# Split weight blocks whose low part comes from an accumulating DMA instead of a subtraction

## The chip, the cores and the metric

One core of one Trainium2 chip runs the whole program in one launch. The metric is the device time of that launch in microseconds; lower is better. The kernel before has three timed runs: 2505.35, 2509.59 and 2516.16 us, median 2509.59.

## What is computed

One inference step of a two-layer backbone on 640 tokens of 1,024 features (128 context tokens and 512 latent tokens). Each layer is a half-step feed-forward, a token mixing and a second half-step feed-forward, each followed by a residual and a layer norm, with shift, scale and gate vectors from two conditions:

```python
def half_ffn(x, shift, scale, gate, w_gate, w_up, w_down, g, b):
    h = modulate(x, shift, scale)
    return post_norm(x, FFN_HALF * swiglu(h, w_gate, w_up, w_down), gate, g, b)

for l in range(DEPTH):
    mc = ada_mods(c_ctx[None, :], w_ada[l], b_ada[l])
    ms = ada_mods(c, w_ada[l], b_ada[l])
    y = half_ffn(y, ...)
    o = ab_mixer(...) if l % 2 == 0 else fourier_mixer(...)
    y = post_norm(y, o, ...)
    y = half_ffn(y, ...)
```

Layer 0 mixes with two attentions (a windowed one and a latent one, with one input and one output projection), layer 1 with a Fourier transform over positions and channels. The hidden width of the feed-forward is 2,816. All data are float32.

## The kernel before

Features lie on the partitions, tokens on the free axis, in two parts of 256 and 384 tokens (later 254 and 386), of which the second goes first. A float32 product is made of three products of TensorE's float32r type: x = hi + lo with hi the rounded value and lo the rest, and w x = w_hi x_hi + w_hi x_lo + w_lo x_hi (`mm3`). So each weight block of 128 x 1,024 floats (512 KB) has to be split into hi and lo before TensorE reads it.

`load_in` takes one of **three raw tiles** (`self.raws`), issues the block's load on SyncE's queue, and starts the generator that `block` returns. That generator has two pieces: a copy of raw to hi, by ScalarE or VectorE, and then lo = raw - hi, by VectorE or GpSimd; behind the subtraction the raw tile is given back, and the pair is filed under its key. The engine of a piece is chosen by estimates (`choose`, with the prices of `copies` and `sums`).

The blocks that go this way are the 176 gate and up blocks of the four feed-forwards (`gu_block`, 44 each), their 88 down blocks, 12 of the attention's input projection and 8 of its output projection: 284. The 128 tiles of w_ada (modulation vectors) pass through the same three raw tiles, but are read in place by VectorE (two instructions CUSTOM_DVE_ANT_0 each). The Fourier mixing splits its blocks in code of its own, which the change leaves as it is.

Names in what follows: `wu` and `w` hold gate and up blocks (at the output projection also the blocks 0 to 3), `wd` down blocks (there the blocks 4 to 7), `wi` and `w` the input projection's; `hh` and `hl` are the high and low parts of the activations, `hd` those of the hidden layer. hi and lo have the same name with consecutive numbers: `wu_8991` is a hi, `wu_8992` its lo.

The order of all work is fixed when the program is written. TensorE's products stand in line (`chain`, `ffn`, `ab_out`); the other engines' pieces are generators that `tick` emits when an estimate of the clock (`Clock`, `Queue`, `Loads`) says that they can start. The engines then work through their queues in that order, each instruction waiting for what it needs. `load_in` may issue a load as soon as a raw tile has been given back in this order; on the chip the load then waits until the last reader of that tile is through.

Places in hi and lo tiles: a feed-forward has room for six gate and up blocks and four down blocks at a time, the output projection for all eight of its own (two are loaded early, during the attention).

Of the kernel before, what the change touches and what calls it, by code (L numbers as in the profile page):

```python
# [24 lines left out]
# The tokens in two parts; features are on the partitions throughout. Up to the attention the prompt and 128 of  # L25
# the sample, and the rest; then the prompt and what meets its mirror image in the sample's first or last 63, and
# the sample's first token and the others. By part: (first column, token among prompt and sample, tokens).
# [16 lines left out]
# Of the scheduling below, in ns: how far ahead of TensorE's queue the other engines' pieces are emitted, what  # L44
# speaks against DVE where a piece can go elsewhere, and what counts as the same time.
# [3 lines left out]
# Units of the two attentions in progress at once.  # L49
UNITS_A, UNITS_B = 6, 4  # L50
# The engines for the first modulation's scale, by tile: TensorE or DVE.
# [3 lines left out]
def pieces(parts, t0, n):  # L55
    """Where the tokens t0 to t0 + n lie: (part, column, tokens before, tokens)."""
    out = []
    for half, runs in enumerate(parts):
        for c, t, m in runs:
            a, b = max(t, t0), min(t + m, t0 + n)  # L60
            if a < b:
                out.append((half, c + a - t, a - t0, b - a))
    return out


class Clock:
    """Estimates in ns: by tile, when it will be written (and by which engine) and when its slot is free."""
# [5 lines left out]
class Pool:  # L73
    """A pool of tiles that notes which tile follows which in a slot; since: when its memory is free at the earliest."""
# [15 lines left out]
    def used(self, name):  # L90
        """When the last tile of that name will be through."""
        return self.clock.used.get(self.rings[name][-1], 0) if name in self.rings else 0


class Slots:
    """Tiles of one shape in a pool, taken and given back in any order."""
# [26 lines left out]
class Queue:  # L123
    """An engine, with an estimate in ns of when it will be through what it has been given."""
# [4 lines left out]
    def __getattr__(self, op):  # L129
        def issue(*args, **kw):  # L130
            aps = [x for x in (*args, *kw.values()) if isinstance(x, bass.AP)]
            out = kw.get("out", args[0] if args else None)
            self.run(aps, [out, kw.get("accum_out")], self.cost(op, args, aps, kw))
            return getattr(self.engine, op)(*args, **kw)  # L134
        return issue

# [13 lines left out]
    def after(self, x):  # L150
        """When tile x can be read."""
# [18 lines left out]
class Loads:  # L170
    """The DMA queue."""
# [14 lines left out]
def sums(n):  # L186
    """What a sum or difference of n columns takes, by the engines that it can go to."""
# [3 lines left out]
def scaled(n, times=1):  # L191
    """Likewise for n columns times a scale by partition plus a shift by partition."""
# [3 lines left out]
def copies(x, times=1):  # L196
    """Likewise for copies of x."""
# [12 lines left out]
def size(x):  # L210
    return int(np.prod(x.shape[1:]))


class Step:
    """Float32 products run as float32r: x = hi + lo with hi rounded to float32r and lo the exact rest,
    w x = w_hi x_hi + w_hi x_lo + w_lo x_hi; or as float32, where the splits would cost more than they spare.

    Instructions are issued in the order of emission. Matrix products are emitted in line; the work of the other
    engines is in generators, whose pieces `tick` emits as they are expected to start. A generator yields the
    engine of its next piece (or None) and what that waits for: a tile, or a condition on what has been emitted."""  # L220

    def __init__(self, ctx, tc, io):
# [7 lines left out]
        # what is put off of a plain normalisation, and how many tiles that leaves  # L230
# [30 lines left out]
    def parted(self, parts):  # L261
        """The tokens' parts from here on: widths, and (column, width, modulation vector), vector 0 c's, 1 c_ctx's."""
# [8 lines left out]
    def ffn_pool(self, ctx):  # L271
        """Its memory was used until now."""
# [7 lines left out]
    def psum(self, ctx):  # L280
        """A stage's banks for the products emitted in line; two more are for the generators."""
        self.banks = Slots(self.pool(ctx, "ps", space=bass.MemoryType.PSUM), "a", 6, [128, 512], F32)

    def spawn(self, gen, on=None, what=None, unit=False, first=0):
        """first: its rank among pieces that can start at the same time."""
        self.side.append([gen, on, what, unit, first])

    def begin(self, on, what):
        """When a piece is expected to start, None if it can't yet."""
# [7 lines left out]
    def choose(self, on, what):  # L297
        """The engine that is expected to be through with a piece first, and when it would start."""
# [8 lines left out]
    def step(self, limit=None, patient=False):  # L307
        """Emit the piece expected to start first; with a limit, only one that keeps to it (by engine)."""
# [9 lines left out]
        try:  # L318
            # a generator that has begun is told which engine
# [18 lines left out]
    def pair(self, n):  # L338
        """Room for two sums of n columns, in one bank where they go there."""
# [31 lines left out]
    def load_in(self, src, use):  # L371
        """Issue a load into a free raw tile; use(tile) then is spawned, or done if it is no generator."""
# [7 lines left out]
    def loader(self, loads):  # L380
        """Loads in turn, each (when it may be issued, source, use)."""
# [4 lines left out]
    def block(self, dst, key, pool, name, bufs):  # L386
        """What turns a loaded block into its (hi, lo), kept in dst[key]."""
        def use(raw):
# [3 lines left out]
            eng = yield sums(size(hi)), hi  # L392
            eng.tensor_tensor(lo, raw, hi.bitcast(F32), ALU.subtract)
            self.raws.give(raw)
# [9 lines left out]
    def products(self, out, parts, hl, start, stop):  # L404
        """out (+)= sum of v x over parts (v, columns of x), the products with x's high part first."""
# [8 lines left out]
    def chain(self, ps, w, xs, tick=True):  # L414
        """ps = sum over k of w[k] (K, M) and xs[k] (K, N), each as (hi, lo)."""
# [7 lines left out]
    def ada_open(self, ctx, early=False):  # L423
        """What the modulation vectors are worked out with: silu of both conditions, on every partition."""
# [29 lines left out]
    def rstd(self, q, n, eps, out, delta=None, banks=None):  # L454
        """out[0] = 1/sqrt(colsum(q)/n + eps), or less (colsum(delta)/n)^2 under the root, broadcast over the
        partitions in a bank; q and delta are given back."""
# [9 lines left out]
        # the last 128 columns overlap those before where need be  # L466
# [24 lines left out]
        # a first guess from the exponent, then three of Newton's steps  # L491
# [17 lines left out]
    def affine(self, i, l, m):  # L509
        """(scale, shift), [128, KT, 2] each, by which the normalised rows become the modulated ones:  # L510
        normalisation i (or none), then the modulation (l, m), (l, m + 1)."""
# [39 lines left out]
    def norm_sum(self, half, o, st, then):  # L551
        """Add output tile o to the sum over the features, in the order of o; after the last go on with then()."""
# [14 lines left out]
    def shifted_sum(self, half, o, st, then):  # L567
        """The same without waiting for all features: what comes of output tile o less the mean m of the first two
        tiles, the sum of the squares and that of the tiles after the first two. With d the mean of all the
        differences, to which the first two tiles add nothing, the variance is the mean square less d^2, and d^2 is  # L570
        at most three times the variance."""
# [24 lines left out]
    def pivot(self, half, st, s):  # L596
        """The sum of the first two tiles' features, from the tiles' sum s."""
# [10 lines left out]
    def square(self, half, st, o, n):  # L608
        """Add the square of ya[o] to the sum of squares st["q"]; with all tiles at once the last ones' sum is in st["part"]."""
# [24 lines left out]
    def norm(self, half, st, i, aff, ag, plain=False, spill=None):  # L634
        """Layer norm i of a part. Then, modulated by aff, the next stage's input, into self.h (plain: not
        split), and in ya (or spill) ALPHA times the normalised rows; without aff, the result."""
# [4 lines left out]
        # at the end there are no products that need the other banks  # L641
        banks = self.banks if aff is None and not held else self.psc
        # the mean, with the tiles shifted already what is left of it
# [75 lines left out]
    def h_split(self, half, o, t, h):  # L719
        """The next stage's input tile from t, which is given back."""  # L720
# [9 lines left out]
    def start(self, pool):  # L730
        """The first input: the modulation's shift by DVE, its scale by TensorE, a tile of features at a time."""
# [15 lines left out]
        # silu of both conditions, on every partition  # L747
# [12 lines left out]
        def weighed(o):  # L760
            # by DVE
# [40 lines left out]
        def rest():  # L802
            for o in range(KT):
                if o + 1 < KT:
                    # among the first blocks of weights
# [11 lines left out]
    def gu_block(self, l, j, n, pool, dst, turn=0):  # L817
        """Loading the n-th block of gate and up weights: 2 f + (0 or 1). Of six in turn two are kept in w."""
# [3 lines left out]
    def ffn(self, l, j, i, nxt, pool, gu, first, turn=0, ada=0, urgent=0, after=(), early=False, **kw):  # L822
        """i: the normalisation that ends it; nxt: the modulation (layer, index) that follows it; gu: the
        first blocks of weights, there or on their way; ada: how many tiles of w_ada to work through, so many of them urgent;
# [1271 lines left out]
```

## Time and profile before

| | |
|---|---|
| median of three runs | 2509.59 us (2505.35 to 2516.16) |
| profiled execution, span from its first to its last instruction | 2503.6 us, 6.0 us below the median |
| TensorE matmul, weight load | 2413.5 us (96%), 2314.1 us (92%) |
| VectorE, ScalarE, GpSimd | 1595.8 us (64%), 723.5 us (29%), 641.9 us (26%) |
| DMA | 259.03 MB, 31.0% of 16 engines' time, mean 103 GB/s |

The profile is one execution. A group's row gives its busy time and the mean of one instruction; the idle time behind the bar is that of the engine just before it, with what ended it. The share of an engine over the whole span is a mean over stages with different limits. PE stands for TensorE's products, PEld for its weight loads, DVE for VectorE, ACT for ScalarE, POOL for GpSimd, SP for SyncE.

### The profile page before, as it was taken

How to read it: one execution, taken by the hardware profiler on the slowest of the kernel's cores; microseconds unless marked ns; L12 is line 12 of the kernel's file. 1: busy time of each engine (PE TensorE's matmuls, PEld its weight loads, DVE VectorE, ACT ScalarE, POOL GpSimd, SP SyncE). 2: the span in 40 equal slices, each digit the busy share in tenths (PEclk: the TensorE clock that was granted, in tenths of full speed). 3: DMA queues.
4: the chain of work that ended last, by engine and by line, in shares of the span. 5: the costliest groups of instructions: out<-in, count | busy, mean ns of one | idle time of the engine just before them, and what ended most of it. 6: DMA issues, size and time to landing. Idle time of an engine off the chain costs nothing. (4 is left out here: it accounts for less than half of the span.)

```text
span 2503.6 us, 39511 instructions
## 1 busy us (share of the span) xinstructions
PE 2413.5 (96%) x15713; PEld 2314.1 (92%) x15713; DVE 1595.8 (64%) x3194; ACT 723.5 (29%) x1475; POOL 641.9 (26%) x499
## 2 busy tenths in 40 slices
PE   7999999989989999999999999999989989999997
PEld 7999999987577999999999999999976879999997
DVE  8867766677567686456566677676687963323346
ACT  3221212254666442112122322211234322221122
POOL 6312221242322152013112421100245522201112
PEclk8999999999899999999999999999999989999998
DMA  6535434140012225134240354443423213112121
GB/s 247 177 118 176 143 118 160 34 135 31 7 36 78 85 84 169 64 122 149 95 136 27 102 174 137 132 147 118 136 81 108 90 43 102 65 63 76 51 76 43
DMA packets 86025, 259.03 MB, mean 103 GB/s; under 512 B 13832, under 2 KB 26824, under 8 KB 85712
## 3 DMA queue, kind: packets, MB, share of 16 engines
q1 hardware_dynamic: 85840, 256.50, 31.0%
q8 instruction: 124, 2.03, 0.3%
q14 instruction: 61, 0.50, 0.1%
HBM read 248.84 MB, written 5.52 MB: 102 GB/s over the span
## 5 line engine op out<-in xcount | busy, mean ns | idle before, releaser
L359 PE MATMUL a<-hh,wu 128*128 128x254 f32 (+3 forms) x3840 | 855.1, 311 | 4.7 <-DVE hh L134 4.6
L359 PEld LDWEIGHTS a<-hh,wu 128*128 128x128 f32 x3840 | 653.4, 190 | 6.7 <-DVE hh L134 5.8
L359 PE MATMUL a<-hd,wd 128*128 128x254 f32 (+3 forms) x4224 | 629.1, 310 | 3.7 <-DVE ya L134 3.4
L359 PEld LDWEIGHTS a<-hd,wd 128*128 128x128 f32 x4224 | 624.2, 189 | 6.7 <-issue 3.7
L359 PE MATMUL a<-hl,wu 128*128 128x386 f32 (+3 forms) x1920 | 597.5, 311 | 3.0 <-POOL hl L134 1.6
L359 PE MATMUL a<-hh,w 128*128 128x254 f32 (+6 forms) x2240 | 504.2, 314 | 1.3 <-ACT hh L134 0.9
L134 DVE CUSTOM_DVE_ANT_0 junk<-raw,cond,bada 128x1024 bf16<-128x1024 f32 x256 | 379.0, 1481 | 12.3 <-DMA raw<-in_w_ada 7.8
L359 PEld LDWEIGHTS a<-hh,w 128*128 128x128 f32 (+1 forms) x2240 | 380.2, 191 | 7.1 <-issue 2.5
L359 PEld LDWEIGHTS a<-hl,wu 128*128 128x128 f32 x1920 | 364.9, 190 | 4.6 <-DVE hl L134 2.2
L134 DVE TENSOR_TENSOR tmp<-tmp,a 128x254 f32<-128x254 f32 (+3 forms) x176 | 85.5, 486 | 430.1 <-PE a L359 420.3
L359 PE MATMUL a<-hl,w 128*128 128x254 f32 (+4 forms) x1056 | 329.8, 312 | 3.0 <-POOL hl L134 2.0
L134 DVE SCALAR_TENSOR_TENSOR ya<-a,gate,ya 128x128 f32<-128x128 f32 (+3 forms) x576 | 226.7, 433 | 145.7 <-PE a L359 144.7
L134 POOL TENSOR_TENSOR wu<-raw,wu 128x1024 fp32r<-128x1024 f32 x55 | 150.4, 2744 | 633.0 <-ACT wu L134 617.0
L134 ACT CAST hd<-tmp 128x386 fp32r<-128x386 f32 (+3 forms) x163 | 75.5, 463 | 513.2 <-DVE tmp L134 513.0
L359 PEld LDWEIGHTS a<-hl,w 128*128 128x128 f32 (+1 forms) x1056 | 200.4, 190 | 6.4 <-POOL hl L134 2.8
L134 POOL TENSOR_TENSOR w<-raw,w 128x1024 fp32r<-128x1024 f32 (+3 forms) x49 | 106.9, 2189 | 357.9 <-ACT w L134 356.8
L134 ACT ACTIVATE tmp<-a 128x254 f32<-128x254 f32 (+3 forms) x176 | 76.8, 437 | 323.3 <-PE a L359 322.6
L134 ACT CAST wu<-raw 128x1024 fp32r<-128x1024 f32 x110 | 113.2, 1047 | 160.4 <-DMA raw<-in_w_gu 122.1
L134 ACT CAST wd<-raw 128x1024 fp32r<-128x1024 f32 x66 | 68.2, 1047 | 254.7 <-PE a L359 153.7
L134 DVE TENSOR_TENSOR hd<-tmp,hd 128x254 fp32r<-128x254 f32 (+3 forms) x152 | 89.3, 588 | 65.2 <-ACT hd L134 64.9
L134 POOL TENSOR_TENSOR wd<-raw,wd 128x1024 fp32r<-128x1024 f32 x22 | 60.4, 2749 | 193.7 <-ACT wd L134 150.8
L134 DVE TENSOR_TENSOR wd<-raw,wd 128x1024 fp32r<-128x1024 f32 x70 | 95.0, 1365 | 10.5 <-ACT wd L134 9.8
(438 smaller groups left out, 2575.8 us busy)
## 6 DMA issues: line engine op xcount, KB each, us to landing
raw<-in_w_gu SPq DMA_DIRECT2D x176, 512.0 KB, 3.7
raw<-in_w_ada SPq DMA_DIRECT2D x128, 512.0 KB, 3.8
raw<-in_w_dn SPq DMA_DIRECT2D x88, 512.0 KB, 3.6
raw<-in_w_fin SPq DMA_DIRECT2D x16, 520.0 KB, 3.8
wd<-in_w_ada SPq DMA_DIRECT2D x16, 512.0 KB, 7.5
raw<-in_w_ab SPq DMA_DIRECT2D x11, 512.0 KB, 3.7
raw<-in_w_abo SPq DMA_DIRECT2D x8, 512.0 KB, 4.3
raw<-in_w_fout SPq DMA_DIRECT2D x8, 512.0 KB, 3.6
```

The source lines that it names most:

```text
L134: return getattr(self.engine, op)(*args, **kw)
L359: pe.engine.matmul(out, w, x, **kw)
```

## The change

The copy of a block to hi stays. The subtraction goes. In its place ScalarE writes -hi into lo, and GpSimd then issues a DMA that adds the block to lo in memory. For the down blocks of the feed-forward (`src` given) the added block is read from DRAM a second time, and the raw tile is given back behind ScalarE's instruction; for all others it is read from the raw tile, which is given back behind the DMA.

```diff
+    def dma_add(self, out, in_):
+        c = self.clock
+        self.run([out, in_], [out], 1000)
+        c.ready[out.tensor.name] = self.t + 3000 + 8e-3 * int(np.prod(out.shape)) / 0.354, "d"
+        c.used[out.tensor.name] = c.used[in_.tensor.name] = c.ready[out.tensor.name][0]
+        return self.engine.dma_start(out=out, in_=in_, accum_op=ALU.add)
...
-    def block(self, dst, key, pool, name, bufs):
+    def block(self, dst, key, pool, name, bufs, src=None):
         def use(raw):
             eng = yield copies(raw), raw
             hi, lo = (pool.tile([128, D], F32R, name=name, bufs=bufs)[:raw.shape[0], :raw.shape[1]] for _ in range(2))
             copy(eng, hi, raw)
-            eng = yield sums(size(hi)), hi
-            eng.tensor_tensor(lo, raw, hi.bitcast(F32), ALU.subtract)
-            self.raws.give(raw)
+            yield "s", hi
+            self.nc.scalar.mul(lo, hi.bitcast(F32), -1.0)
+            if src is not None:
+                self.raws.give(raw)
+            yield "g", lo
+            self.nc.gpsimd.dma_add(lo, raw if src is None else src)
+            if src is None:
+                self.raws.give(raw)
             dst[key] = hi, lo
         return use
...
-                todo.append((t0, use[kind, n - 4][1] + 1 if n >= 4 else 0, io["w_dn"][l, j, n], self.block(dn, n, pool, "wd", 8)))
+                todo.append((t0, use[kind, n - 4][1] + 1 if n >= 4 else 0, io["w_dn"][l, j, n], self.block(dn, n, pool, "wd", 8, io["w_dn"][l, j, n])))
```

Since the estimates differ, pieces also move: of the 300 copies of raw blocks VectorE had 43 and has 148, and GpSimd's queue has 284 DMA issues where it and VectorE had 113 and 171 subtractions. TensorE's order stays the same in kind.

GpSimd at the start of the program, before (`raw0` to `raw2` hold gate and up blocks, `ya` the input, `mod` modulation vectors, `tmp` the modulated input):

```order
L134 TENSOR_SCALAR ya1_0_122<-ya1_0_122 128x384
L134 TENSOR_SCALAR ya0_0_114<-ya0_0_114 128x256
L134 TENSOR_SCALAR ya1_1_123<-ya1_1_123 128x384
L134 TENSOR_SCALAR tmp3_264<-ya0_1_115,mod0_1_161,mod0_0_160 128x128 x2
L134 TENSOR_SCALAR ya0_1_115<-ya0_1_115 128x256
L134 TENSOR_TENSOR hl0_1_282<-tmp3_264,hh0_1_281 128x256
```

The same place with the change:

```order
L134 TENSOR_SCALAR ya0_0_114<-ya0_0_114 128x256
L143 DMA wu_214<-raw0_177 128x1024
L134 TENSOR_SCALAR ya1_1_123<-ya1_1_123 128x384
L134 TENSOR_SCALAR tmp3_265<-ya0_1_115,mod0_1_161,mod0_0_160 128x128 x2
L134 TENSOR_SCALAR ya0_1_115<-ya0_1_115 128x256
L143 DMA wu_260<-raw1_185 128x1024
```

The low parts of the first two blocks were VectorE's; now their DMAs stand in GpSimd's queue, each behind the scaling of an input tile.

GpSimd where the attention ends and the output projection begins, before (`p` is the last softmax, `lns` a sum of the layer norm that follows):

```order
L134 TENSOR_SCALAR p2_8777<-p2_8777,st_8734 128x640
L134 TENSOR_SCALAR p0_8832<-p0_8832,st_8786 128x640
L134 TENSOR_TENSOR wu_8992<-raw0_8902,wu_8991 128x1024
L134 TENSOR_TENSOR lns0_9054<-lns0_9054,ya0_3_8911 128x254
L134 TENSOR_TENSOR lns1_9244<-lns1_9244,tmp0_9264 128x254
```

With the change:

```order
L134 TENSOR_SCALAR p0_8912<-p0_8912,st_8866 128x640
L143 DMA wu_9072<-raw2_8982 128x1024
L143 DMA wu_9078<-raw1_8984 128x1024
L143 DMA wd_9087<-raw0_8986 128x1024
L134 TENSOR_TENSOR lns0_9127<-lns0_9127,ya0_2_8990 128x254
L143 DMA wd_9167<-raw2_9110 128x1024
L143 DMA wd_9184<-raw1_9123 128x1024
L143 DMA wd_9208<-raw0_9134 128x1024
```

All six blocks that the projection still has to load are now added by DMAs, the last three through the raw tiles of the first three. ScalarE at the same place, with the change:

```order
L134 ACTIVATE cond_8976<-cond_8976 128x2048
L134 CAST wu_9077<-raw1_8984 128x1024
L134 ACTIVATE wu_9072<-wu_9071 128x1024
L134 ACTIVATE wu_9078<-wu_9077 128x1024
L134 ACTIVATE wd_9087<-wd_9086 128x1024
L134 ACTIVATE wd_9167<-wd_9166 128x1024
```

The first negation stands behind ScalarE's activation of `cond` and its copy of the second block; before, the copy was followed by the copy of the fourth block `wd`.

## Rows read from the trace of the kernel before

**Rows 1.** The page: busy time of each engine.
```profile
PE 2413.5 (96%) x15713; PEld 2314.1 (92%) x15713; DVE 1595.8 (64%) x3194; ACT 723.5 (29%) x1475; POOL 641.9 (26%) x499
```
**Rows 2.** Stretches inside the four feed-forwards: busy us, clock, DMA share, GB/s.
```profile
100.00:450.00 350.00, 350.00 (x2392) 350.00 (x2391) 244.39 (x379) 74.80 (x110) 76.82 (x28) 1.00 0.43 143
950.00:1350.00 400.00, 400.00 (x2684) 400.00 (x2683) 222.32 (x364) 82.16 (x121) 74.48 (x30) 1.00 0.35 113
1400.00:1800.00 400.00, 400.00 (x2726) 399.95 (x2727) 280.06 (x454) 89.51 (x140) 71.08 (x36) 1.00 0.42 139
2050.00:2450.00 400.00, 400.00 (x2682) 400.00 (x2681) 135.07 (x246) 79.04 (x118) 56.21 (x21) 1.00 0.21 68
```
**Rows 3.** Stretches between and around them, same view and columns.
```profile
0.00:50.00 50.00, 38.11 (x209) 37.37 (x210) 37.59 (x54) 15.99 (x33) 29.02 (x28) 0.80 0.80 298
...
1350.00:1400.00 50.00, 45.73 (x307) 43.71 (x305) 41.77 (x101) 22.85 (x42) 29.84 (x26) 0.97 0.22 69
...
2000.00:2050.00 50.00, 37.91 (x199) 36.03 (x198) 39.02 (x79) 15.26 (x29) 16.93 (x14) 0.80 0.20 64
```
**Rows 4.** Groups by line: a subtraction on either engine, a copy on ScalarE and VectorE.
```profile
L134 POOL TENSOR_TENSOR wu<-raw,wu 128x1024 fp32r<-128x1024 f32 x55 | 150.4, 2744 | 633.0 <-ACT wu L134 617.0 <-PE a L359 6.5 <-DVE wu L134 6.4
...
L134 ACT CAST wu<-raw 128x1024 fp32r<-128x1024 f32 x110 | 113.2, 1047 | 160.4 <-DMA raw<-in_w_gu 122.1 <-PE a L359 24.9 <-issue 13.4
...
L134 DVE TENSOR_TENSOR wu<-raw,wu 128x1024 fp32r<-128x1024 f32 x65 | 85.2, 1313 | 23.7 <-ACT wu L134 23.4
...
L134 DVE CAST wd<-raw 128x1024 fp32r<-128x1024 f32 x26 | 19.7, 760 | 16.1 <-DMA raw<-in_w_dn 15.8
```
**Rows 5.** DMA issues: name, queue, count, KB, median us from issue to landing.
```profile
raw<-in_w_gu SPq DMA_DIRECT2D x176, 512.0 KB, 3.7
...
raw<-in_w_abo SPq DMA_DIRECT2D x8, 512.0 KB, 4.3
```
**Rows 6.** Timeline of VectorE, then tile wu on TensorE: the tightest block of 100 to 450.
```profile
404.73 1.23 DVE L134 TENSOR_TENSOR wu<-raw,wu 128x1024 fp32r<-128x1024 f32 x1
...
L359 PE MATMUL a<-hh,wu x13: 331/337/341, 416.7 to 419.8; 128*128 128x384 f32 x13
```
**Rows 7.** Timelines where the output projection begins: ScalarE, GpSimd, TensorE, SyncE's queue.
```profile
840.50 1.93 ACT L134 ACTIVATE cond<-cond 128x2048 f32<-128x2048 f32 x1
842.33 1.03 ACT L134 CAST wu<-raw 128x1024 fp32r<-128x1024 f32 x1
...
841.49 2.81 POOL L134 TENSOR_TENSOR wu<-raw,wu 128x1024 fp32r<-128x1024 f32 x1 [6.36 <-DVE wu L134]
...
844.20 0.28 PE L359 MATMUL a<-hh,wu 128*128 128x254 f32 x1
844.32 0.28 PE L359 MATMUL a<-hl,wu 128*128 128x254 f32 x1
844.43 0.43 PE L359 MATMUL a<-hh,wu 128*128 128x254 f32 x2
...
849.86 0.28 PE L359 MATMUL a<-hh,wd 128*128 128x254 f32 x1
...
844.33 2.55 SPq L183 DMA_DIRECT2D raw<-in_w_abo  x3
```
**Rows 8.** Timelines of the start: GpSimd, then TensorE.
```profile
11.70 0.51 POOL L134 TENSOR_SCALAR ya<-ya 128x384 f32<-128x384 f32 x1
...
18.27 1.42 POOL L134 TENSOR_SCALAR ya<-ya 128x384 f32<-128x384 f32 x1 [3.95 <-DVE tmp L134]
...
23.57 1.25 POOL L134 TENSOR_SCALAR ya<-ya 128x256 f32<-128x256 f32 x1
...
23.08 0.84 PE L359 MATMUL a<-hh,wu 128*128 128x384 f32 x2
...
36.05 0.44 PE L359 MATMUL a<-hh,wu 128*128 128x384 f32 x1 [2.73 <-DVE hh L134]
38.10 0.69 PE L359 MATMUL a<-hl,wu 128*128 128x384 f32 x1 [1.60 <-POOL hl L134]
```

## Prediction

> **What bounds the kernel now.** The page first: TensorE is busy 96% of the span, VectorE 64%, ScalarE and GpSimd under 30% [rows 1]. Then the stretches: inside the four feed-forwards TensorE and its weight loads are busy for the whole of 1,550 us, at the full clock (1.00, the 2.4 GHz level) [rows 2]. Relief of VectorE or GpSimd is worth nothing there. All that TensorE idles is 2503.6 - 2413.5 = 90.1 us, in the start, the mixings and the norms three of these places are shown [rows 3]. So the change can save little; it can cost wherever a low part now comes after TensorE wants it.
>
> **What the change removes and adds.** Out go 284 subtractions, 1.31 us on VectorE or 2.74 us on GpSimd each [rows 4]. In come 284 negations on ScalarE, which I price as its copy of the same shape, 1.05 us, and 284 DMA issues. 105 copies go from ScalarE (1.05 us) to VectorE (0.76 us) [rows 4]. ScalarE gains 284 x 1.05 - 105 x 1.05 = 188 us and comes to some 36% of the span; it waits most of that time already, so I charge this only where its queue stands before a DMA (below). VectorE loses 171 x 1.31 - 105 x 0.76 = 144 us.
>
> **The unknown price** is T, from GpSimd's issue of an accumulating DMA to its landing. No row of before has one, nor any DMA from GpSimd. The nearest is a load of the same 512 KB from SyncE, 3.7 us [rows 5]. Below: T = 3.7, one transfer (a gain against a load is excluded, since the same bytes are read and written and more). Above: 11.1 us, three transfers in a row, for two reads and one write. I take 7.4 us, two transfers, since twice the bytes are read and as many written. What GpSimd's queue itself spends on an issue is taken as part of T.
>
> **Inside the feed-forwards** I charge nothing. The cover is the lead of a block over its use. The tightest block that I found from 100 to 450 us has its subtraction end at 405.96, and the first product that reads its lo starts at 417.04, the third of the block's first products [rows 6]: 11.1 us. The new way adds 1.05 + 7.4 - 1.23 = 7.2 us. With T at 11.1 it adds 10.9 and the cover is gone. The same blocks hold their raw tile longer by this much, the down blocks shorter. Behind a GpSimd issue that waits for ScalarE stand the hidden layer's few splits that GpSimd has, with leads of their own.
>
> **The output projection, 840 to 861 us**, is where no lead exists. Before, GpSimd ended the third block's low part at 844.30, and TensorE read it in the product at 844.43 [rows 7]. Now ScalarE stands in the way: it activates `cond`, copies the fourth block until 843.36, and only then negates the third, to 844.41. The DMA lands at 844.41 + T, so TensorE waits T. Then the raw tile: the third block's tile is free at 844.41 + T, not at 844.33, when SyncE issued the next loads [rows 7]. The sixth block's load takes 4.3 [rows 5], its copy 0.76, its negation 1.05, its DMA T: ready at 850.5 + 2T. TensorE takes (849.86 - 844.20) / 2 = 2.83 us for a block [rows 7] and would come to this low part at 844.43 + T + 3 x 2.83 = 852.9 + T. It waits T - 2.4 again. The seventh and eighth follow through two more tiles and are then in time. Together 2T - 2.4: 12.4 us at 7.4, 5.0 at 3.7, 19.8 at 11.1. TensorE has no idle time right behind that would take it up.
>
> **The start.** The second block's DMA stands in GpSimd's queue behind the scaling of input tiles, which ended at 23.57 + 1.25 = 24.82; TensorE read this low part at 23.08 [rows 8]. The wait is 24.8 + T - 23.1 = 1.7 + T; of it TensorE's two later waits for activations, 2.73 and 1.60 us, take up 4.3 [rows 8]. Left: T - 2.6, 4.8 us at 7.4, 1.1 to 8.5 at the ends. The DMA engines run at a share of 0.80 in the first 50 us [rows 3], so T may be longer there; on the other side VectorE, 75% busy, loses some subtractions. I leave these two against each other.
>
> One row speaks for GpSimd being slow at this place: the same scaling takes 0.51 us at 11.70 and 1.42 at 18.27 [rows 8], with VectorE at work beside it. The Trainium skill (SBUF — State Buffer, the note on the trap that DVE blocks DMA) says that descriptors of a DMA issued by GpSimd are written by GpSimd itself, that a two-port VectorE copy locks it out meanwhile, and gives 620 ns alone against some 3,100 beside a copy. By that rule, as an estimate, T would be 2.5 us longer wherever VectorE copies, and the sum 7.5 us more.
>
> **Relief.** In the stretches at 1350 and 2000 TensorE idles 4.3 and 12.1 us with VectorE 78 to 84% busy [rows 3]; few blocks fall there. I take 2 us off.
>
> **Sum.** (2T - 2.4) + (T - 2.6) - 2 = 3T - 7.0: 15.2 us at 7.4 (4.1 at 3.7, 26.3 at 11.1). The profiled span 2503.6 becomes 2518.8; it lies 6.0 below the median, so I say **2525 us**. A measurement of this kernel tells about 0.5%, 12.5 us, from no change: faster is below 2497, slower above 2522.
>
> **Rivals.**
>
> *Not slower: T is near a load's.* For it: an idle transfer engine, and all waits shrink with T (4.1 us at 3.7): 2514. The two sides meet at T = 6.5. Against it: two reads and a second queue. The Trainium skill (DMA: Bandwidth & Descriptors, on the anatomy of a DMA issued by GpSimd) fits 2.0 us plus bytes over 436 GB/s; for two reads of 512 KB that is an estimate of 4.4 us, and by it the sum would be 6.2 us, 2516. No run here has shown such a DMA yet.
>
> *The transfer engines fill up.* From 100 to 450 us the loads' share is 0.43 at 143 GB/s [rows 2], or 143 x 350 / 524 = 95.5 blocks, 0.43 x 350 / 95.5 = 1.58 us of all engines each. TensorE's 2,392 products there [rows 2] are 50 blocks at 48 each. At two loads' time an accumulation adds 50 x 3.15 / 350 = 0.45, total 0.88: it fits. It decides from (1 - 0.43) x 350 / 50 = 4.0 us, 2.5 loads, on (T about 9.3, sum 21, 2530). At three loads, 4.7 us, the four stretches come to 1.11, 1.01, 1.10 and 0.87 the same way, with 56, 57 and 56 blocks in the last three [rows 2], 37 + 6 + 38 = 81 us over, and with 26.3 from above 2617. The middle is 2574. For it: SyncE's three raw tiles would be held longer at the same time. Against it: the lead of 11 us and more.
>
> *Faster.* VectorE and GpSimd were late at the start and in the norms, and the leads at the two places are regained: with a third of the 11.9 + 4.3 + 12.1 us of idle time [rows 3] back and no wait, 2509.6 - 9 = 2500; 2495 if half. Against it: most of these waits are for norms, not for blocks.
>
> **How the numbers follow.** The forecast 0.45 (2519 to 2537), full engines 0.20, T near a load's 0.27, faster 0.08. The range reaches from 2508 to 2595; outside lie most of the faster case and the upper end of the engines' case, some 0.15. Slower: nine tenths of the forecast's 0.45, and 0.20, together 0.60; faster 0.07; the same 0.33. The forecast's own range is 2519 to 2537.
>
> **What would show it.** Right: T near 7 us in the list of issues; TensorE's waits for DMAs to `wu` and `wd` just behind the attention, some 7 and 5 us; one wait of some 10 us near 23 us; the four stretches of rows 2 still full. Wrong: idle time of TensorE inside a feed-forward with a DMA share near 1 (full engines), or both places without waits (short T). A T under 5 or over 9 makes the number wrong even if the places are right.

## The result and the profile after

The changed kernel takes **2625.66 us** (four runs, 2618.1 to 2632.14) against 2509.35 before: a ratio of 1.0452, with a 95% interval from 1.0420 to 1.0485. The forecast was 2525, the range 2508 to 2595. The direction was right, the size and the range were not.

The page of the profiled execution: span 2630.4 us, then busy times, the two DMA queues that carry the blocks, and the time to landing of the largest groups of issues.

```profile
PE 2453.0 (93%) x15713; PEld 2342.3 (89%) x15713; DVE 1369.2 (52%) x3154; ACT 891.1 (34%) x1623; POOL 562.4 (21%) x675
...
q0 software_dynamic: 40896, 148.52, 31.0%
q1 hardware_dynamic: 85840, 256.50, 28.5%
...
raw<-in_w_gu SPq DMA_DIRECT2D x176, 512.0 KB, 5.3
...
wu<-raw POOLq DMA_DIRECT2D x120, 512.0 KB, 6.2
...
wd<-in_w_dn POOLq DMA_DIRECT2D x88, 512.0 KB, 10.4
```

Against [rows 1], TensorE's busy time has grown by 39.5 us and its idle time from 90.1 to 177.4, by 87.3; that is the whole difference of the spans, 126.8. TensorE does the same products: its mean granted clock fell from 0.978 to 0.959. The accumulating DMAs are all that the queue q0 holds, and 0.310 x 2630.4 / 284 = 2.87 us: that is what one addition costs of all 16 transfer engines. A gate or up load takes 5.3 us to land where it took 3.7 [rows 5].

What TensorE waited for, the first three of that view (total us, times, longest):

```profile
PE a L367 <- DMA wu<-raw: 61.3, 17, 10.1
PE a L367 <- DMA w<-raw: 18.8, 7, 7.4
PE psc L367 <- POOL lns L134: 9.6, 4, 4.6
```

Most of the new idle time ends with an addition's landing, and none with that of a feed-forward's down block. The interiors of the feed-forwards, which answer to [rows 2], in the same columns (length; busy time and instructions of PE, PEld, DVE, ACT, POOL; clock, DMA share, GB/s):

```profile
94.00:468.00 374.00, 367.88 (x2498) 366.61 (x2497) 203.19 (x383) 103.00 (x137) 54.32 (x58) 0.99 0.76 200
1012.00:1378.00 366.00, 362.88 (x2418) 361.97 (x2417) 167.51 (x326) 97.62 (x132) 47.47 (x51) 1.00 0.71 179
1504.00:1891.00 387.00, 373.79 (x2498) 372.48 (x2497) 206.85 (x394) 106.69 (x149) 56.90 (x65) 0.98 0.76 198
2173.00:2546.00 373.00, 370.60 (x2499) 370.28 (x2498) 99.78 (x216) 108.96 (x142) 48.09 (x54) 1.00 0.62 148
```

TensorE is no longer full there, at DMA shares of 0.62 to 0.76.

To see where the 126 us lie, I cut both traces at the same numbers in TensorE's sequence of 15,713 products, and took the time from the start of one such product to that of the next. "Inside" is the sum of the four feed-forwards without their first and last blocks (products 400 to 2900, 5680 to 8100, 8800 to 11300, 12800 to 15300); "seams" is the start, the joints around the first three feed-forwards with their norms and the input projection, and the output projection; then the attention, the stretch from the Fourier mixing to the start of the last feed-forward, and the end. The table has all runs of this study, in us.

```
                                inside   seams  attention  Fourier..4th    end
before                          1458.5   521.2      280.3         161.1   70.6
after                           1501.6   620.0      282.5         139.0   74.9
e1  four raw tiles              1461.6   611.3      293.0         136.5   70.6
e2  before, four raw tiles      1458.6   537.6      297.0         149.8   70.6
e3  gate/up added from DRAM     1467.2   584.4      285.5         144.8   70.7
e4  down blocks subtracted      1462.3   599.7      280.2         137.7   70.7
e5  seam blocks subtracted      1498.4   521.9      281.2         142.3   70.3
e6  e5 + added from DRAM        1466.8   526.5      282.4         147.2   70.6
e7  DMAs in the 4th only        1460.7   519.3      280.9         137.2   73.5
e8  copy without addition       1460.8   557.9      282.6         139.1   70.6
e9  12 DMAs before the 4th      1460.9   524.6      284.0         136.5   69.9
e10 these 12 on VectorE         1458.5   522.6      282.3         164.1   70.6
e11 all added from raw tiles    1524.0   633.4      280.1         145.0   76.5
e12 all on VectorE              1458.4   518.7      282.6         163.9   70.6
```

After against before: **seams +98.8, inside +43.1**, attention +2.2, end +4.3, and **-22.1** before the fourth feed-forward.

### The profile page after: what moved, and what is told of

Read it like the earlier page. It is cut to its first block, busy times and chain, and to the rows that moved or that the text cites. A ratio compares the mean times of both kernels' runs of the same rounds, so it can differ in the third digit from the quotient of the medians.

```text
span 2630.4 us, 40065 instructions
## 1 busy us (share of the span) xinstructions
PE 2453.0 (93%) x15713; PEld 2342.3 (89%) x15713; DVE 1369.2 (52%) x3154; ACT 891.1 (34%) x1623; POOL 562.4 (21%) x675
## 5 line engine op out<-in xcount | busy, mean ns | idle before, releaser
L367 PE MATMUL a<-hh,wu 128*128 128x254 f32 (+3 forms) x3840 | 878.8, 318 | 71.2 <-DMA wu<-raw 61.3
L367 PEld LDWEIGHTS a<-hh,wu 128*128 128x128 f32 x3840 | 669.4, 195 | 78.8 <-DMA wu<-raw 67.0
L134 DVE CUSTOM_DVE_ANT_0 junk<-raw,cond,bada 128x1024 bf16<-128x1024 f32 x256 | 330.8, 1292 | 197.7 <-DMA raw<-in_w_ada 193.6
L134 DVE SCALAR_TENSOR_TENSOR ya<-a,gate,ya 128x128 f32<-128x128 f32 (+2 forms) x576 | 231.0, 435 | 193.1 <-PE a L367 190.1
L143 POOL DMA_DIRECT2D wu<-raw x120 | 108.9, 919 | 731.5 <-ACT wu L134 590.5
L134 ACT ACTIVATE wu<-wu 128x1024 fp32r<-128x1024 f32 x120 | 126.9, 1060 | 206.6 <-DVE wu L134 193.7
L143 POOL DMA_DIRECT2D wd<-in_w_dn x88 | 82.1, 951 | 303.4 <-ACT wd L134 236.7
L143 POOL DMA_DIRECT2D w<-raw x66 | 58.8, 894 | 369.6 <-ACT w L134 282.8
L134 ACT ACTIVATE wd<-wd 128x1024 fp32r<-128x1024 f32 x92 | 97.1, 1060 | 90.9 <-DVE wd L134 89.8
L134 ACT CAST wu<-raw 128x1024 fp32r<-128x1024 f32 x67 | 69.7, 1040 | 90.2 <-DMA raw<-in_w_gu 83.9
## 6 DMA issues: line engine op xcount, KB each, us to landing
wd<-in_w_dn POOLq DMA_DIRECT2D x88, 512.0 KB, 10.4
```

Source lines behind the costliest of these rows:

```text
L143: return self.engine.dma_start(out=out, in_=in_, accum_op=ALU.add)
L367: pe.engine.matmul(out, w, x, **kw)
```

## The experiments

Two theories were to be told apart for the inside, and a third for the rest. **Ring**: the three raw tiles are always taken, so each is refilled when the addition that reads it has landed, and longer additions mean fewer blocks. **Engines**: the transfer engines carry too much. **Late blocks**: at the seams a low part is ready only just before TensorE wants it, and each added microsecond is waited for.

**e1, a fourth raw tile, and e2, its control.** The room comes from one softmax tile of the latent attention.

```diff
-        self.raws = Slots(self.pool(ctx, "raw"), "raw", 3, [128, RAW], F32)
+        self.raws = Slots(self.pool(ctx, "raw"), "raw", 4, [128, RAW], F32)
...
-        pps = Slots(p, "p", 3, [128, 640], F32)
+        pps = Slots(p, "p", 2, [128, 640], F32)
```

> The changed kernel with four raw tiles instead of three (one softmax tile of the latent attention is given up for the room, so the attention may be a few us longer). Ring theory: inside the feed-forwards TensorE waits because each gate and up block holds its raw tile 17 to 22 us from load to landed addition (11 to 17 before) and all three tiles are always taken. A fourth gives a third more room, so the waits for DMAs to wu and w (83 us in all, some 50 of them inside the three feed-forwards that also load w_ada) drop to about 35, what is left being the start, the output projection and the first blocks of a feed-forward: 2550 to 2575 us. Engine theory: the transfer engines, at a share of 0.65 to 0.9 there, are what is short; a fourth tile moves no byte less: 2610 to 2635. Late-blocks theory (all the loss at the places without a lead): 2615 to 2630.

> The kernel before with four raw tiles and one softmax tile less, as control of the run above. TensorE had no idle time inside the feed-forwards, so the fourth tile should be worth nothing there, at most some us at the start and the norms: 2500 to 2515 by each theory. A gain of 15 us or more would mean that the ring already cost time before.

Measured: e1 2587.54 us, e2 2527.34. The total of e1 lies between the theories, and e2 is 12 us above its range (1.0079, 1.0049 to 1.0108, of before). The missing softmax tile cost more than I allowed: the attention of e2 is 17 us longer than before, and its seams 16 us; before the fourth feed-forward it gains 11 us. So outside the feed-forwards e1 is no clean test. The inside decides, and there e2 is like before. In e1 it is 1461.6: all but 3 us of the 43 are regained, with the transfer engines as busy as with the change. Two of e1's four interiors:

```profile
93.00:456.00 363.00, 363.00 (x2493) 363.00 (x2492) 194.98 (x372) 111.00 (x143) 48.35 (x54) 1.00 0.76 206
...
1489.00:1855.00 366.00, 366.00 (x2486) 366.00 (x2485) 208.90 (x403) 115.93 (x159) 55.34 (x64) 1.00 0.77 208
```

At shares of 0.76 and 0.77 TensorE has no gap. So full transfer engines were not what it waited for inside; it was room in the ring. The seams hardly gained (611.3).

**e3, gate and up blocks added from DRAM**, so that the raw tile is free behind the negation.

```diff
-        return self.io["w_gu"][l, j, n // 2, n % 2], self.block(dst, n, *own)
+        return self.io["w_gu"][l, j, n // 2, n % 2], self.block(dst, n, *own, self.io["w_gu"][l, j, n // 2, n % 2])
```

> The gate and up blocks, too, are added from DRAM a second time, so that their raw tile is given back behind the negation and not behind the DMA. Three raw tiles. Ring theory: the hold of a gate or up block falls from 17 to about 9 us, the waits inside the feed-forwards go (some 50 us with their clock), though each addition takes 10 us instead of 6: 2570 to 2600. Engine theory: as many bytes through the same engines, so the waits stay, and the longer additions add to them: 2620 to 2680.

Measured: 2566.12 us, just below the range of the ring theory and far from that of the engines. Three tiles and as many bytes, and the inside is 1467.2. In the first feed-forward a gate or up block holds its tile 10.1 us on average from the issue of its load to its last reader's end; it was 10.7 before and 16.8 with the change. The seams gain 36 us too, 20 of them where the second feed-forward starts.

**e4, down blocks by subtraction again.**

```diff
-  ... self.block(dn, n, pool, "wd", 8, io["w_dn"][l, j, n])))
+  ... self.block(dn, n, pool, "wd", 8, sub=True)))
```

> The 88 down blocks go back to a subtraction on VectorE or GpSimd; gate, up and projection blocks stay with the DMA from the raw tile. Engine theory: a third of the additions' engine time goes (88 x 2.98 us of 815 us), share inside the feed-forwards down by 0.12, so most waits inside go: 2570 to 2590. Ring theory: the down blocks now hold their raw tile 7 us instead of 5.7, gate and up ones as long as with the change, less the fuller engines: little better or none, 2600 to 2630.

Measured: 2568.09 us, just below the range of the engine theory and far from that of the ring, inside 1462.3. The two theories are not as separate as I had put them: with a third of the additions gone, the loads land in 4.5 us instead of 6.1, and a gate or up block holds its tile 15.7 us instead of 16.8, a w_ada tile 10.0 instead of 10.6. So the engines' load counts, too; that it does so by the time that it adds to each hold is my reading of these means.

**e5, subtraction for the blocks without a lead; e6, the same with the rest added from DRAM.** The calls for the input and the output projection get `sub=True`, which brings the subtraction back; those of gate and up blocks get it by number:

```diff
...
-        ... self.block(dst, n, *own)
+        ... self.block(dst, n, *own, sub=n >= 40 or (l, j) != (1, 1) and n < 8)
```

> The changed kernel, but with a subtraction for the blocks whose low part came less than some 15 us ahead of TensorE before: the input and output projection's (20), gate and up blocks 0 to 7 of the first three feed-forwards and 40 to 43 of all four (40). 224 additions stay, three raw tiles. Local theory: outside the interiors of the feed-forwards the change lost some 96 us between the same products of TensorE (15 start, 22 end of the first feed-forward and input projection, 12 output projection, 23 start of the second, 12 and 14 around the third) and won 22 between the Fourier mixing and the fourth; nearly all of the loss goes, the 43 us inside remain in good part: 2530 to 2555. Ring theory alone (all waits from the three raw tiles, wherever they show): the ring is relieved by a seventh only, 2585 to 2610.

> As the run above, and the gate and up blocks that are still added by a DMA are added from DRAM, so that the raw tile is given back behind the negation. If the loss is the sum of waits inside (ring) and of late blocks at places without a lead, both are now away: 2490 to 2520, with the 22 us won before the fourth feed-forward perhaps kept. If the transfer engines have a price of their own, 2540 or more.

Measured: e5 2529.15 us, e6 2506.28 (ratio 0.9980, 0.9968 to 0.9993). With 60 blocks back, the seams are at 521.9, as before the change, and the inside is still 1498.4. So the seams' loss was made by these 60 blocks, and it is separate from the inside. e6 takes away both, and 224 additions by DMA then cost nothing in sum: 8 us inside and 5 at the seams are paid for by 14 before the fourth feed-forward.

**e8, the addition left out.**

```diff
-        return self.engine.dma_start(out=out, in_=in_, accum_op=ALU.add)
+        return self.engine.dma_start(out=out, in_=in_)
```

> The changed kernel with the addition left out of the DMA: a plain copy overwrites lo with the block, so the products are wrong, while instructions, order and number of DMAs are the same. It prices the addition itself. If an accumulation costs two reads and a write against one and one, the engines' time for each falls from 2.9 to about 1.5 us and T from 6.2 (raw tile) to 4 to 5 us; waits inside the feed-forwards go, 2560 to 2590. If the price is GpSimd's issue and the order alone, T and the time stay: 2610 to 2630.

Measured: 2527.57 us (one run), better than either range, with these rows for queue and landing:

```profile
q0 software_dynamic: 40896, 148.52, 17.0%
...
wu<-raw POOLq DMA_DIRECT2D x120, 512.0 KB, 3.7
wd<-in_w_dn POOLq DMA_DIRECT2D x88, 512.0 KB, 7.2
```

0.170 x 2525.8 / 284 = 1.51 us of all engines each, against 2.87: the addition nearly doubles the price, in the engines as in T (3.7 against 6.2). The inside is as before the change (1460.8). The order of the work alone, with as many DMAs, still costs 37 us at the seams, of which the 22 before the fourth feed-forward give most back.

**e11, the hold made longer.** Down blocks, too, are added from the raw tile (`src` is left out of their call).

> The changed kernel, with the down blocks too added from the raw tile, which is given back behind the DMA and not behind the negation. As many DMAs and bytes, three raw tiles. Ring theory: 88 blocks hold their tile some 8 us longer, 66 of them in the three full feed-forwards, 66 x 8 / 3 = 176 us more of ring time where it is full already: 2680 to 2800. Engine theory: the same transfers, those from the raw tile even land sooner (6 us against 10): 2600 to 2640.

Measured: 2670.78 us, 45 us over the change; inside 1524.0. As the ring theory says, not the engine theory, though below its range: a down block's hold in the first feed-forward rises from 5.7 to 13.4 us, but the additions from the raw tile burden the loads less, and a gate or up block's falls from 16.8 to 15.1.

**e7 and e9, where the 22 us come from, and a version that beats both.** e7 adds by DMA only in the last feed-forward, e9 only its first 12 blocks.

```diff
e7
...
+        ... self.block(dst, n, *own, sub=(l, j) != (1, 1))
...
e9
...
+        ... self.block(dst, n, *own, sub=(l, j) != (1, 1) or n >= 8)
+        ... self.block(dn, n, pool, "wd", 8, io["w_dn"][l, j, n], (l, j) != (1, 1) or n >= 4)
```

> Subtractions as before everywhere but in the last feed-forward, whose 44 gate and up and 22 down blocks are added by DMAs as in the change. There no w_ada tile passes through the ring, and the change itself lost 5 us inside and won 22 in the stretch that leads to it, where TensorE waited for VectorE's sums of the norm (9.7 us in one place). If that gain comes from VectorE being free of this feed-forward's subtractions: 2485 to 2500, faster than both. If it came from the work being later by 100 us anyway (another phase of the w_ada tiles): 2505 to 2515.

> Subtractions as before, except for the first 8 gate and up blocks and the first 4 down blocks of the last feed-forward, which are added by DMAs (12 DMAs in all). If the gain before that feed-forward (161 to 137 us between the same products) is made by these blocks alone, it is kept, and the 2 us lost inside and 3 at the end of the run with all 66 blocks come back: 2482 to 2492. If it needs VectorE to be free of the later blocks too: 2495 to 2510.

Measured: e7 2493.44 us (0.9921, 0.9901 to 0.9940), **e9 2488.62 us (0.9916, 0.9892 to 0.9940)**, both faster than before by 0.8%; the intervals do not tell them apart. The gain before the fourth feed-forward is kept by 12 DMAs. Before, VectorE and GpSimd there (timelines):

```profile
1988.89 6.31 DVE L134 SCALAR_TENSOR_TENSOR ya<-tmp,mod,ya 128x194 f32<-128x194 f32 x4
...
1998.53 4.49 DVE L134 SCALAR_TENSOR_TENSOR ya<-tmp,mod,ya 128x194 f32<-128x194 f32 x2
...
1989.65 5.00 POOL L134 TENSOR_TENSOR w<-raw,w 128x1024 fp32r<-128x1024 f32 x2
1997.91 4.90 POOL L134 TENSOR_TENSOR wd<-raw,wd 128x1024 fp32r<-128x1024 f32 x2 [3.25 <-ACT wd L134]
...
2015.20 1.65 PE L359 MATMUL psc<-lns,onem 128*128 128x386 f32 x2 [9.67 <-DVE lns L134]
```

In e9 at the same place:

```profile
1988.82 1.79 DVE L134 SCALAR_TENSOR_TENSOR ya<-tmp,mod,ya 128x194 f32<-128x194 f32 x4
...
1994.56 0.86 POOL L143 DMA_DIRECT2D w<-raw  x1
```

Four instructions of VectorE took 6.31 us beside two of GpSimd's subtractions, and 1.79 without them; the sum `lns` that TensorE waited 9.67 us for stands behind them in VectorE's queue. In e9 TensorE's longest wait from 1969 to 2021 us is 0.5 us.

**e10 and e12, the same without DMAs.** The 12 blocks (e10), or all 284 (e12, without the condition `v`), are subtracted on VectorE alone.

```diff
-            eng = yield sums(size(hi)), hi
+            eng = yield {"v": 0} if v else sums(size(hi)), hi
```

> The kernel before, without any added DMA, with the same 12 blocks subtracted on VectorE alone, where some were GpSimd's. Contention theory: VectorE's operations with two SBUF inputs take 1.6 to 2.6 us beside a subtraction on GpSimd and 0.3 to 0.5 us otherwise, and it is these, in the norm before the last feed-forward, that TensorE waits for; without GpSimd's subtractions there the stretch shortens although VectorE has more to do: 2485 to 2500. Load theory (the gain was VectorE's and GpSimd's work being less): VectorE has some 6 subtractions of 1.2 us more in the norm: 2510 to 2525.

> The kernel before with all 284 subtractions on VectorE, none on GpSimd, no added DMA. Contention theory: VectorE gets 113 x 1.23 = 139 us more, in stretches where it waits for TensorE most of the time, and loses the stretching of its operations beside GpSimd's: 2485 to 2505. Load theory: VectorE goes from 64 to 69% busy and is later at the starts and norms: 2515 to 2540.

Measured: e10 2511.76 us (1.0016, 1.0000 to 1.0032), e12 2509.28 (0.9997, 0.9979 to 1.0015): no gain, and the stretch is 164.1 and 163.9 us long. The contention theory failed as I had put it; e10 is in the range of the load theory, e12 between the two. The stretched instructions are gone, but the low parts now come late, from VectorE's queue; in e10:

```profile
1997.33 0.80 PE L359 MATMUL a<-hh,wu 128*128 128x254 f32 x2 [8.58 <-DVE wu L134]
```

So, as far as these runs show, the gain needs both: no subtraction on GpSimd beside the norm, and none in VectorE's queue that TensorE then waits for. That is what a DMA gives. These blocks on GpSimd alone were not tried, and a DMA is not the only way to part of it: e2, which has none, is 11 us shorter here, with a longest wait for `lns` of 4.3 us.

## Why the prediction was wrong, and where it was right

**The output projection** was right in its places, and in its number by luck. The waits are where they were named (timelines of ScalarE, GpSimd, TensorE and SyncE's queue, as [rows 7]):

```profile
893.45 2.00 ACT L134 ACTIVATE wu<-wu 128x1024 fp32r<-128x1024 f32 x2
...
894.81 1.80 POOL L143 DMA_DIRECT2D wu<-raw  x2 [9.47 <-ACT wu L134]
...
899.48 0.79 PE L367 MATMUL a<-hh,wu 128*128 128x254 f32 x2 [4.60 <-DMA wu<-raw]
...
913.83 0.51 PE L367 MATMUL a<-hh,wd 128*128 128x254 f32 x2 [3.43 <-DMA wd<-raw]
...
899.49 7.01 SPq L191 DMA_DIRECT2D raw<-in_w_abo  x3
```

The first wait is T, the second what the raw tile's late return leaves, and the loads go out at 899.49, when the first addition has landed. T was 4.6 here, where 7.4 had been taken, so the formula 2T - 2.4 gives 6.8. The two waits are 8.0, and the stretch was 12.5 us longer (33.9 against 21.4), where 12.4 had been forecast. The other 4.5 are slower products, which the sum had no term for, and they happen to make up for the shorter T: the clock, 1.00 before at this place, was granted at 0.84 and 0.89 behind the waits.

```profile
899.50:914.00 14.50, 11.07 (x73) 10.86 (x74) 4.48 (x11) 3.17 (x3) 3.31 (x4) 0.84 0.93 219
914.00:930.00 16.00, 16.00 (x105) 15.95 (x106) 6.43 (x19) 2.21 (x7) 0.73 (x1) 0.89 0.61 155
```

Over the whole span idle time explains 87 us, and the products at a lower clock the other 39.5.

**T, taken as 7.4**, is 6.2 in the middle for blocks from raw tiles, between 4.4 (the least of 196) and 15.0; from DRAM it is 10.4, which "T" as one number had not told apart. The fitted price of the Trainium skill (DMA: Bandwidth & Descriptors, on the anatomy of a DMA issued by GpSimd) gave an estimate of 4.4 us for two reads; that is the least measured, and no middle of a loaded kernel. The rule of the Trainium skill weighed beside it (SBUF — State Buffer, the trap that VectorE blocks GpSimd's DMAs, by which T was estimated to be 2.5 us longer) hardly shows: an issue took 1.09 us on average where it met one of VectorE's copies of raw blocks (52) and 0.89 otherwise (232), and the middle T of the blocks from raw tiles was 5.0 us with such a copy and 6.3 without.

**"Inside the feed-forwards I charge nothing. The cover is the lead of a block"** is the first step that failed: 43.1 us, shown by e1 and e3 to be room in the three raw tiles. A lead covers one late block. It does not cover each block being late by more than the one before because its load could go out only when a tile came back; I wrote that the raw tiles are held longer, and gave it no price. In the first feed-forward the mean hold of 36 gate and up blocks rose from 10.7 to 16.8 us, that of w_ada tiles (43 and 41) fell from 12.2 to 10.6 and of 18 down blocks from 7.9 to 5.7. Holds times blocks, divided by the three tiles, make an estimate of what the ring needs: 351 us before and 381 with the change. TensorE took 364 us for this stretch before and 374 with the change. For e3, e4 and e8 the same sum is 358 to 359, and they took at most 2.1 us longer than before; for e11 it is 374, and it took 381. It is a rough check, made from holds that were measured afterwards. That the ring had no room to give was there to be read in SyncE's queue: before, 1,205 us of its waits for a tile ended with a subtraction (375.0, 239.3 and 205.8 on VectorE for `wu`, `w`, `wd`, 186.8, 142.6 and 55.1 on GpSimd) and 527 with w_ada's last reader. After:

```profile
SPq L191 <- DMA wu<-raw: 709.3, 112, 42.8
SPq L191 <- DVE mod L134: 430.9, 113, 18.4
SPq L191 <- DMA w<-raw: 348.4, 57, 34.8
```

The fourth feed-forward, with as many blocks but no w_ada tiles, lost 5 us, the others 10, 6 and 22.

**"The output projection ... is where no lead exists"** is the second, and the larger: I looked for the tightest block only from 100 to 450 us and charged two places. The seams lost 98.8 us, 12.5 of it there, and e5 shows that the lateness of 60 blocks made it. Outside 100 to 450 the trace of before had leads of 0.7 and 2.8 us for two blocks near 75 us, of 2.2 for one block of the input projection and 7.3 to 9.6 for four others, and of 9.5 and 8.6 at the start of the third feed-forward; each stood ready to be read as the output projection's was. The worst one does not come from a lead alone. At the start of the second feed-forward (ScalarE, GpSimd, TensorE):

```profile
964.03 1.06 ACT L134 ACTIVATE wu<-wu 128x1024 fp32r<-128x1024 f32 x1 [12.88 <-DVE wu L134]
...
987.64 0.86 POOL L143 DMA_DIRECT2D wu<-raw  x1
...
992.25 0.80 PE L367 MATMUL a<-hh,wu 128*128 128x254 f32 x2 [10.07 <-DMA wu<-raw]
```

The negation was done at 965.1, the DMA issued 22.5 us later: it stood in GpSimd's queue behind the norm's sums and scalings, which wait for VectorE. I had looked at what stands behind a DMA in this queue, and at what stands ahead only at the start. That this place was lost to the queue, and not to T, e8 bears out, where the same order meets a T of 3.0 us (ScalarE, GpSimd, TensorE):

```profile
918.45 1.06 ACT L134 ACTIVATE wu<-wu 128x1024 fp32r<-128x1024 f32 x1 [8.86 <-DVE wu L134]
...
942.55 0.60 POOL L143 DMA_DIRECT2D wu<-raw  x1
...
945.59 0.79 PE L367 MATMUL a<-hh,wu 128*128 128x254 f32 x2 [8.50 <-DMA wu<-raw]
```

The DMA again goes out 23 us behind the negation, and of the 22.6 us that the change lost around this place e8 still loses 16.2. The queue was not changed alone (e3 and e5 both mend this place, one by earlier loads, one by subtractions).

**The start.** The second DMA was issued at 19.66 us and not at 24.8. The first two additions took 9.6 and 8.5 us, with the transfer engines full (DMA shares of 1.04 and 1.05 in these stretches), and were waited for 2.04 and 3.53 us, where one wait of some 10 had been named; the two activations' waits of [rows 8] took this up, and at 43 us TensorE was where it had been before. So the term of 4.8 us was 0 net. The loss of 15.5 us by 97 us came later, from the blocks near 75 us: a wait of 8.69 us that ended at 86.92. The addition that it waited for was issued at 74.16, as the fourth within 5.2 us, and took 12.7 us to land.

**Relief, taken as 2 us**, was 22.1: TensorE's idle time in the stretch went from 17.7 to 4.1 us, and its products took 8.4 us less at a higher clock (0.92 before, 0.99 after). I priced it by the few blocks that fall there; it lay in the norm's instructions on VectorE, which GpSimd's subtractions had stretched, and in the clock, which had no term.

**The rivals.** "The transfer engines fill up" came nearest by its number (up to 2617), but not by its mechanism: an addition cost 2.87 us of the engines where it was to decide from 4.0 on, the shares stayed at 0.62 to 0.76 (0.88 had been worked out for the first feed-forward), and e1 has 0.76 and 0.77 in two of its interiors without a gap. What filled up was the raw tiles. "T is near a load's" was near the least T, and even at T = 3.7 (e8) the time is 17 us above before, with seams 37 us longer.

## What to carry to other kernels

Where a transfer replaces an instruction, price what it holds while it is under way: hold time times blocks, divided by the tiles in the ring, against the length of the whole stage, and not only the lead of the tightest block. Then list every block with a short lead at the starts and ends of stages, and look up in the issuing engine's queue what stands ahead of its transfer. A transfer was worth most here where both engines that could do the work were needed by a norm at that moment: 12 of the 284 carried the gain.

## What the runs showed of the hardware that I had not expected

VectorE's instructions that read two operands from SBUF are held up by a subtraction on GpSimd. In the kernel before, `hd<-tmp,hd` took 2.63 us on average in the 7 cases beside one, and 0.49 in the 138 with GpSimd idle; `ya<-tmp,mod,ya` took 1.64 and 0.31; `ya<-a,gate,ya`, which reads one operand from PSUM, took 0.44 in both. In e12, where GpSimd has no subtraction of a block, `hd<-tmp,hd` took 0.49 with GpSimd idle and 0.45 beside its other work. The tile `hd` on VectorE, before and then after (least, middle and most, ns):

```profile
L134 DVE TENSOR_TENSOR hd<-tmp,hd x152: 408/550/2639, 65.7 to 2474.9; 128x254 fp32r<-128x254 f32 x63, 128x386 fp32r<-128x386 f32 x53, 128x256 fp32r<-128x256 f32 x19, 128x384 fp32r<-128x384 f32 x17
```

```profile
L134 DVE TENSOR_TENSOR hd<-tmp,hd x150: 410/426/905, 65.8 to 2601.0; 128x254 fp32r<-128x254 f32 x61, 128x386 fp32r<-128x386 f32 x55, 128x384 fp32r<-128x384 f32 x17, 128x256 fp32r<-128x256 f32 x17
```

The Trainium skill says so (SBUF — State Buffer, section "SBUF: two separate sides"): a VectorE instruction with two SBUF inputs and a GpSimd instruction that reads SBUF take a shared pair of ports in turn, each for its whole length. The trace agrees; I had drawn on the page for a rule against the change, and not for this one, which speaks for it.

Accumulating DMAs issued close together landed one after the other. At the output projection, three issued from 894.81 to 896.69 us landed 4.6, 6.3 and 9.4 us after their issue, 2.6 and 4.0 us apart, where one takes an estimated 2.87 us of all engines. In the whole trace 25 pairs of additions from raw tiles were issued within 1.3 us of each other, and landed 3.5 us apart in the middle (2.4 to 6.5); in e8, without the addition, 23 such pairs landed 1.5 us apart.
